# Two-part weights of a hybrid decoder trunk, made by transfers within SBUF

## Chip, cores, metric

One core of a Trainium2 chip runs the whole kernel in one launch. The metric is the device time of that launch in microseconds (us); the kernel before takes 1227.74 us (median of 2 runs, 1227.51 to 1227.97).

## What is computed

The reference is a decoder trunk of two layers on 512 tokens with 1024 features, all in float32:

```
for l in range(DEPTH):                                   # DEPTH = 2
    proj = rms_norm(h, g_mix[l]) @ w_in[l]               # 1024 x 2560: q | k | v | xr | gr
    ... differential attention of 4 heads on q, k, v     -> o
    ... causal convolution, RG-LRU scan on xr, GELU(gr)  -> y
    h = h + concatenate([o, y]) @ w_out[l]               # 1024 x 1024
    hm = rms_norm(h, g_mlp[l])
    h = h + square(relu(hm @ w_mlp_in[l])) @ w_mlp_out[l]    # 1024 x 4096, 4096 x 1024
    gate = sigmoid(rms_norm(h, g_ple[l]) @ w_ple_gate[l])    # 1024 x 1024
    h = h + gate * (p[l] @ w_ple_proj[l])                # 256 x 1024
return rms_norm(h, g_final)
```

## The kernel before

**Numbers in two parts.** TensorE multiplies in the type fp32r, which keeps fewer bits than float32. Every operand is therefore split into a part `hi`, rounded to fp32r, and a part `lo`, the rest. One product of float32 numbers is three fp32r products: hi by hi, hi by lo, lo by hi (`mm3`).

**Weights.** They come as 206 chunks of [128, 1024] float32 (512 KB, 4 KB in each partition), in the order of their use (`chunk_list`): per layer 21 for the input projections and the recurrent gates, 8 for the output projection, 64 for the MLP, 10 for the per-layer embedding. The first two are loaded by halves (`w_half`); the other 204 go through `w_dma`, a load on SP's queue into one of 4 buffers `raw`. `w_split` turns a chunk into `wh` and `wl`, of which there are 6 buffers each. For the chunks of the MLP's first product (`up`) it calls `pair_parts`: that product follows Strassen's method over two output tiles, so VectorE first makes three sums `s1`, `s2`, `s4` of [128, 512] and rewrites half of the second chunk in place; then the two chunks and the three sums are split, the sums into tiles `sh` and `sl` from the general pool of 57 tiles.

In both places ScalarE writes `hi` (a Copy that rounds to fp32r) and VectorE writes `lo = src - hi`. Each chunk's `raw` buffer is free for the next load once `lo` is written, and `wh`, `wl` are free once TensorE has used them.

**Stages of a layer.** x branch (4 chunks and the gates), v (4), four heads (q and k, 8), gate branch (4), output projection (8), then the MLP in four quarters of the hidden features. A quarter has an up stage (8 chunks, 4 pairs, 7 products of halves each) and a down stage (8 chunks, 192 matmuls of 512 columns). The per-layer embedding ends the layer.

**Order.** All instructions are recorded first, with a cost each, and put in order by a list schedule (`Plan.schedule`): each engine takes the oldest recorded instruction that is ready by the modelled times. Every engine's queue, POOL's and SP's among them, then runs in that order, and an instruction that waits holds up what stands behind it on its queue. The plan takes a transfer to occupy its issuing queue 0.47 us and all transfers to share one stream of 355 bytes per ns. All recorded instructions carry line 182 in the profile, so tiles tell them apart. POOL issues no transfer in this kernel; after the set-up it computes the small powers for the norms (`rT`, `orT`).

Of the kernel before, what the change touches and what calls it, by code (L numbers as in the profile page):

```python
# [11 lines left out]
F32 = mybir.dt.float32  # L12
F32R = mybir.dt.float32r
I32 = mybir.dt.int32
AF = mybir.ActivationFunctionType
# [10 lines left out]
NQ = KF // KD  # L26
ORDER = (0, 4, 1, 5, 2, 6, 3, 7)     # output tiles, so that the halves of the features that Strassen pairs come together
HS = S // 2
# [4 lines left out]

# buffers
TB = 57     # tiles of [128, 512]
AT = 2      # tiles for the probabilities of a head, transposed
RAW = 4     # weight chunks as loaded
WB = 6      # weight chunks, split
SC = 4      # PSUM banks that scores may hold

# chunks split ahead in the MLP's products
UA = 2
DA = 2

# the list schedule
WIN = 600   # instructions beyond the oldest one not issued that it may choose from
EV = 150    # boost of what frees PSUM
LP = 600    # how far the norm's sums are put off
RE = -50    # boost of the rotary tables
SW = 2      # us that an instruction waits at most for others that need no new activation table  # L50
SF = 8      # free tiles from which on no check for deadlock is needed
WU = 8      # products that warm up the tensor engine
NM = 4      # output tile of the first up product after which the norm's scale is computed

# [11 lines left out]
class Plan:  # L66
    """Records instructions and issues them in the order of a list schedule: each engine takes, of what is ready,
    what was recorded first (less its boost)."""

# [114 lines left out]
    def schedule(self):  # L184
# [36 lines left out]
        def safe(i):  # L221
            """Whether all that is older than the newest instruction issued can still find its tiles in program order."""
            need = {}
# [132 lines left out]

# columns of the packed per-feature vectors
VCOL = {}
# [16 lines left out]
def chunk_list():  # L375
    """Weight chunks of [128, 1024] in the order in which they are used."""
    c = []
    for l in range(DEPTH):
        c += [("in", l, 12 + m) for m in range(2)]
        c += [("gates", l, 0)]  # L380
        c += [("in", l, 12 + m) for m in range(2, 4)]
        c += [("v", l, i) for i in range(4)]
        for h in range(NH):
            c += [("in", l, h), ("in", l, 4 + h)]
        c += [("in", l, 16 + m) for m in range(4)]
        c += [("out", l, m) for m in ORDER]
        for q in range(NQ):
            c += [("up", l, q * KD + m) for m in range(KD)]
            c += [("down", l, m, q) for m in ORDER]
        c += [("proj", l, 0)]  # L390
        c += [("gate", l, m) for m in range(4)]
        c += [("proj", l, 1)]
        c += [("gate", l, m) for m in range(4, 8)]
    return c
# [6 lines left out]
def build(ctx: ExitStack, tc: tile.TileContext, given, x, p, pos, w, vec, lamqk, out):  # L401
# [25 lines left out]

    # ---------------- weights: streamed, split into two parts that add up exactly
    raw_t, w_t = {}, {}
# [3 lines left out]
    def w_half(i, c):  # L433
        """Half a chunk, for the products that come first."""
        t, hi, lo = T("w0"), T("w0h", F32R), T("w0l", F32R)
        nc.sync.dma_start(out=t, in_=w[i][:, c * S:(c + 1) * S])
        w_t.setdefault(i, []).append((hi, lo))
        nxt["dma"] = nxt["split"] = i + 1
        return t, hi, lo

    def w_dma(j):
        while nxt["dma"] <= min(j, len(CHUNKS) - 1):
# [4 lines left out]
            nxt["dma"] += 1  # L447

    def w_split(j):
        while nxt["split"] <= min(j, len(CHUNKS) - 1):  # L450
# [9 lines left out]
            lo = nc.tile(wsp, [128, 1024], F32R, "wl", WB, "wl")  # L460
            act(out=hi, in_=raw, func=AF.Copy)
            ve.tensor_tensor(out=lo, in0=raw, in1=hi.bitcast(F32), op=ALU.subtract)
            w_t[i] = (hi, lo)
            nxt["split"] += 1

    def pair_parts(a1, a2):
        """The seven weight operands of Strassen's product (Winograd's form) for two output tiles."""
        lft, rgt = slice(0, S), slice(S, 2 * S)
# [6 lines left out]
        for src, n in ((a1, 2), (a2, 2), (s2, 1), (s1, 1), (s4, 1)):  # L475
# [3 lines left out]
            else:  # L479
                hi, lo = T("sh", F32R), T("sl", F32R)  # L480
            act(out=hi, in_=src, func=AF.Copy)
            ve.tensor_tensor(out=lo, in0=src, in1=hi.bitcast(F32), op=ALU.subtract)
            parts += [(hi[:, i * S:(i + 1) * S], lo[:, i * S:(i + 1) * S]) for i in range(n)]
# [22 lines left out]
    def split(src, hi, lo):  # L506
        """src (SBUF or PSUM) into hi + lo."""
        act(out=hi, in_=src, func=AF.Copy)
# [9 lines left out]

    # ---------------- constants
    vt = const.tile([128, NV], F32, name="vt")  # L520
# [21 lines left out]
    def warm_up():  # L542
        """Products of zeros that bring the tensor engine to its full clock while the first loads run."""
        z = T("z", F32R)
# [15 lines left out]
    def rope_setup():  # L560
        """cos and signed sin of the angles, feature-major, 1 and 0 on the rows that don't rotate."""
        posf = T("posf")[:, 0:NT]
# [6 lines left out]
        NA = NT * 16  # L569
        # ang = hi + lo, 1/(2 pi) as a sum of 12-bit parts: every product is exact  # L570
        rest, parts = 1.0 / (2.0 * math.pi), []
# [58 lines left out]
    def vec_setup():  # L630
        for l in range(DEPTH):
            act(out=hb[:, l, 0:4], in_=vt[:, VCOL["b_gate_a", l]:VCOL["b_gate_a", l] + 4], func=AF.Copy, scale=0.5)
            act(out=hb[:, l, 4:8], in_=vt[:, VCOL["b_gate_x", l]:VCOL["b_gate_x", l] + 4], func=AF.Copy, scale=0.5)
            act(out=gsub[:, l:l + 1], in_=V("g_subln", l), func=AF.Copy, scale=1.0 - lam_init(l))
        # softplus(-x) = max(-x, 0) + log1p(exp(-|x|)), the log1p as 2 atanh(y / (2 + y))
        n = DEPTH * 4
# [18 lines left out]
        ve.tensor_scalar(out=sp4n.rearrange("p l t -> p (l t)"), in0=s, scalar1=-4.0, scalar2=None, op0=ALU.mult)  # L655
        # lambda of the differential attention, on every partition
        lq = T("lq")
# [11 lines left out]

    # ---------------- norms: h times its gain goes into the products, 1/rms after them  # L670
    class Norm:
# [20 lines left out]
        def stats(self, square=False):  # L692
            """1/rms (or its square), token-major, and spread over the partitions."""
            ps = PS("msq")
# [24 lines left out]
    class FinalNorm:  # L719
        """The last norm, on each half of the tokens as soon as that is complete."""  # L720

# [35 lines left out]
    def group(ws, rhs, nk, done, late=0, mid=None, tk=slice(0, S)):  # L757
        """ws: per output tile a function giving the chunk slices of K tile k. The last `late` K tiles come last."""
        pss_ = [PM("dense") for _ in ws]
# [16 lines left out]

    # ---------------- one layer
    def layer(l, h, nm, last):
        hg = lambda k: nm.hg[k]
        gate_w = [None]  # L780
        scan_o = [None] * 4
        yo = [None] * KD     # 0..3 attention heads, 4..7 recurrent tiles

# [4 lines left out]

        # recurrent branch
        lru = [dict() for _ in range(4)]  # L790
# [68 lines left out]

        # x branch  # L860
        ws = [take_in(12), take_in(13)]
# [8 lines left out]

        # v, token-major
        pv = [PM("pv") for _ in range(NT)]
# [19 lines left out]

        # attention
        mask_sh = [(i ^ 8) if i < 16 else i for i in range(32)]

        def rope_done(ps, dst):
# [6 lines left out]
            if not dst:  # L903
                # q: per component, its hi part on its own rows and its lo part on the other's
                x0, x1 = T("qx", F32R), T("qx", F32R)
# [5 lines left out]
            else:  # L911
                # k: per component, its hi part on both, and its lo part on its own rows
                y0, y1, lo = T("ky", F32R), T("ky", F32R), T("kl", F32R)
# [115 lines left out]

        # gate branch  # L1030
        for t in range(4):
            group([take_in(16 + t)], hg, KD, lambda i, ps: gr_done(t, ps))

        # output projection; the recurrent tiles come first, the last head last
        order = [4, 5, 6, 7, 0, 1, 2, 3]

        nm2 = Norm("g_mlp", l)
        bp = [dict() for _ in range(4)]     # Strassen's operands of h times its gain, per pair of feature tiles
        fp, t4s = [None] * KD, []
        fat = [AT, []]  # L1040

        def BT(name):
            """512 columns of a tile like those that hold a head's probabilities, as long as there are any."""
            if not fat[1] and fat[0]:
# [40 lines left out]

        # MLP in quarters of the hidden features; the first product by Strassen's method over pairs of output tiles,
        # halves of the input features and halves of the tokens
        nm3 = Norm("g_ple", l)
# [73 lines left out]

        # per-layer embedding
        nmn = None if last else Norm("g_mix", l + 1)
# [18 lines left out]
        def ple(ms, ws, tk, done, **kw):  # L1183
            """proj and gate products of the output tiles ms on the tokens tk."""
            pj = []
# [93 lines left out]
def _layout(i):  # L1279
    """Lays the arrays out as the launch reads them."""  # L1280
    a = {k: np.asarray(v) for k, v in i.items()}
# [59 lines left out]
```

## Time and profile before

| | us |
|---|---|
| median of 2 runs | 1227.74 |
| span of the profiled execution, first to last instruction | 1225.4 |
| PE busy (matmuls) | 1210.8 |
| VectorE busy | 949.0 |
| ScalarE busy | 654.8 |
| POOL busy | 21.4 |

The span is 2.3 us short of the median of the runs; the rest lies around the first and the last instruction. Busy times are those of one profiled execution. A matmul's duration in the profile overlaps the next one's, so the pace of TensorE is read from a stretch and its count of matmuls, not from the mean duration.

### The profile page before, as it was taken

What the parts mean: (1) busy time and instruction counts of PE and PEld (TensorE: products, weight loads), DVE (VectorE), ACT (ScalarE), POOL (GpSimd) and SP (SyncE); (2) the same over time, 40 slices, a digit from 0 to 9 for tenths busy, and PEclk for the clock granted to TensorE, in tenths of its full rate; (3) what the DMA queues carried; (4) which work ended last, traced back from release to release, by engine and by line L of the source; (5) the groups of instructions that cost most, each with busy time, mean ns of one, the idle gap of its engine ahead of it and who ended that gap; (6) DMA issues with size and microseconds to landing.
All of it is one profiled execution on the core that took longest, in us unless ns stands there. A gap on an engine that the chain in (4) does not pass through costs nothing.

```text
span 1225.4 us, 17658 instructions
## 1 busy us (share of the span) xinstructions
PE 1210.8 (99%) x6848; PEld 1049.7 (86%) x6848; DVE 949.0 (77%) x1642; ACT 654.8 (53%) x1068; POOL 21.4 (2%) x43
## 2 busy tenths in 40 slices
PE   8999999999999999999999999999999999999996
PEld 6877788998988989988888777889899899898886
DVE  9898889987777678575778888799776787786564
ACT  6875557743543535543458566576445354355352
POOL 1000000000000000000000000000000000000000
PEclk9999999999999999999999999999999999999998
DMA  6321133243332333332323111223433333343202
GB/s 234 103 69 52 52 89 101 85 124 100 106 103 90 118 93 114 103 103 87 104 69 118 55 35 52 75 81 107 134 103 104 91 104 97 91 136 103 86 1 69
DMA packets 34371, 114.71 MB, mean 94 GB/s; under 512 B 3952, under 2 KB 6000, under 8 KB 34288
## 3 DMA queue, kind: packets, MB, share of 16 engines
q1 hardware_dynamic: 34288, 113.59, 30.2%
q8 instruction: 54, 0.88, 0.3%
q14 instruction: 29, 0.24, 0.1%
HBM read 111.48 MB, written 2.10 MB: 93 GB/s over the span
## 4 chain that ended last, share of the span: by engine, by line
PE 94%; DVE 3%; ACT 1%; DMA 0%; issue 0%; POOL 0%; SPq 0%; POOLq 0%; DVEq 0%; ACTq 0%
PE dense L182 55%; PE up L182 26%; PE sc L182 4%; PE pv L182 2%; PE pj L182 2%; PE av L182 1%; PE bc L182 1%; PE tr L182 1%; PE msq L182 1%; PE osm L182 0%; PE gates L182 0%; DMA h<-x 0%; DVE hs L182 0%; DVE a L182 0%; ACT ky L182 0%
## 5 line engine op out<-in xcount | busy, mean ns | idle before, releaser
L182 ACT ACTIVATE wh<-raw 128x1024 fp32r<-128x1024 f32 x204 | 214.3, 1057 | 279.6 <-PE dense L182 151.8
L182 DVE TENSOR_TENSOR wl<-raw,wh 128x1024 fp32r<-128x1024 f32 x204 | 247.6, 1218 | 22.4 <-ACT wh L182 22.0
L182 PE MATMUL dense<-ffh,wh 128*128 128x512 f32 x512 | 199.5, 390 | 0.0
L182 PE MATMUL dense<-ffl,wh 128*128 128x512 f32 x512 | 199.4, 389 | 0.0
L182 PE MATMUL dense<-ffh,wl 128*128 128x512 f32 x512 | 199.2, 389 | 0.0
L182 PE MATMUL dense<-hgh,wl 128*128 128x512 f32 (+1 forms) x400 | 151.3, 378 | 0.0
L182 PE MATMUL dense<-hgh,wh 128*128 128x512 f32 (+1 forms) x400 | 151.1, 378 | 0.0
L182 PE MATMUL dense<-hgl,wh 128*128 128x512 f32 (+1 forms) x400 | 150.3, 376 | 0.0
L182 PEld LDWEIGHTS dense<-ffh,wl 128*128 128x128 f32 x512 | 96.1, 188 | 20.0
L182 PEld LDWEIGHTS dense<-ffh,wh 128*128 128x128 f32 x512 | 96.1, 188 | 19.8
L182 PEld LDWEIGHTS dense<-ffl,wh 128*128 128x128 f32 x512 | 96.2, 188 | 19.5
L182 ACT ACTIVATE sh<-s 128x512 fp32r<-128x512 f32 x96 | 59.9, 628 | 78.1 <-DVE s L182 77.6
L182 DVE TENSOR_TENSOR dn<-dense,rbc 128x512 f32<-128x512 f32 x64 | 44.2, 690 | 72.7 <-PE dense L182 71.9
L182 PE MATMUL up<-bl,wh 128*128 128x256 f32 x352 | 99.6, 283 | 0.0
L182 PE MATMUL up<-bh,wl 128*128 128x256 f32 x352 | 99.6, 283 | 0.0
L182 PE MATMUL up<-bh,wh 128*128 128x256 f32 x352 | 99.5, 283 | 0.0
L182 PEld LDWEIGHTS dense<-hgl,wh 128*128 128x128 f32 x400 | 75.5, 189 | 12.1
L182 PEld LDWEIGHTS dense<-hgh,wl 128*128 128x128 f32 x400 | 75.5, 189 | 11.9
L182 PEld LDWEIGHTS dense<-hgh,wh 128*128 128x128 f32 x400 | 75.5, 189 | 11.8
L182 PE MATMUL up<-bl,sh 128*128 128x256 f32 x288 | 81.5, 283 | 0.0
L182 PE MATMUL up<-bh,sl 128*128 128x256 f32 x288 | 81.5, 283 | 0.0
L182 PE MATMUL up<-bh,sh 128*128 128x256 f32 x288 | 81.3, 283 | 0.0
(236 smaller groups left out, 2572.0 us busy)
## 6 DMA issues: line engine op xcount, KB each, us to landing
raw<-w SPq DMA_DIRECT2D x204, 512.0 KB, 3.6
h<-x SPq DMA_DIRECT2D x8, 256.0 KB, 5.4
out<-fin SPq DMA_DIRECT2D x8, 256.0 KB, 2.4
w<-w SPq DMA_DIRECT2D x4, 256.0 KB, 4.5
pT<-p SPq DMA_DIRECT2D x4, 256.0 KB, 4.0
lq<-lamqk SPq DMA_DIRECT2D x1, 256.0 KB, 7.1
vt<-vec SPq DMA_DIRECT2D x1, 61.0 KB, 2.4
posi<-pos SPq DMA_DIRECT2D x1, 2.0 KB, 3.0
```

The lines of the kernel that those rows point to most:

```text
L182: d["fn"](*d["args"], **d["kw"])
```

## The change

A new function `w_parts` takes the place of the two instructions of a split, for every chunk and every Strassen sum that was split in `w_split` and `pair_parts`. POOL issues a transfer from the source to `hi` that converts float32 to fp32r; ScalarE writes `lo = -src`, rounded to fp32r; POOL issues a second transfer that adds the source to `lo` in place. VectorE's subtraction is gone. The first two chunks (`w_half`) and all activations keep the old split. The rest of the diff only takes comments away.

```diff
+    def w_parts(src, hi, lo):
+
+        nc.gpsimd.dma_start(out=hi, in_=src)
+        act(out=lo, in_=src, func=AF.Copy, scale=-1.0)
+        nc.gpsimd.dma_start(out=lo.bitcast(F32), in_=src, accum_op=ALU.add)
...
     def w_split(j):
...
             lo = nc.tile(wsp, [128, 1024], F32R, "wl", WB, "wl")
-            act(out=hi, in_=raw, func=AF.Copy)
-            ve.tensor_tensor(out=lo, in0=raw, in1=hi.bitcast(F32), op=ALU.subtract)
+            w_parts(raw, hi, lo)
...
     def pair_parts(a1, a2):
...
                 hi, lo = T("sh", F32R), T("sl", F32R)
-            act(out=hi, in_=src, func=AF.Copy)
-            ve.tensor_tensor(out=lo, in0=src, in1=hi.bitcast(F32), op=ALU.subtract)
+            w_parts(src, hi, lo)
```

## Rows read from the trace of the kernel before

**Rows 1.** The profile's page: busy time of each engine and its share of the span.

```profile
PE 1210.8 (99%) x6848; PEld 1049.7 (86%) x6848; DVE 949.0 (77%) x1642; ACT 654.8 (53%) x1068; POOL 21.4 (2%) x43
```

**Rows 2.** The page: chain that ended last, by engine and by line.

```profile
PE 94%; DVE 3%; ACT 1%; DMA 0%; issue 0%; POOL 0%; SPq 0%; POOLq 0%; DVEq 0%; ACTq 0%
PE dense L182 55%; PE up L182 26%; PE sc L182 4%; PE pv L182 2%; PE pj L182 2%; PE av L182 1%; PE bc L182 1%; PE tr L182 1%; PE msq L182 1%; PE osm L182 0%; PE gates L182 0%; DMA h<-x 0%; DVE hs L182 0%; DVE a L182 0%; ACT ky L182 0%
```

**Rows 3.** Windows: both MLPs whole, then an up and a down stage of layer 0.

```profile
core 0: us, PE busy (x) PEld busy (x) DVE busy (x) ACT busy (x) POOL busy (x), PEclk, DMA share, GB/s
217.77:555.11 337.34, 337.34 (x2130) 307.23 (x2129) 255.65 (x387) 164.53 (x245) 0.00 (x0) 1.00 0.34 105
817.32:1154.57 337.25, 337.25 (x2129) 307.22 (x2129) 255.53 (x386) 165.22 (x245) 0.00 (x0) 1.00 0.34 105
...
303.53:343.84 40.31, 40.31 (x337) 40.31 (x337) 30.53 (x50) 21.57 (x34) 0.00 (x0) 1.00 0.36 111
343.84:387.39 43.55, 43.55 (x194) 36.04 (x194) 31.46 (x43) 17.00 (x24) 0.00 (x0) 1.00 0.29 91
```

**Rows 4.** Groups of instructions: the splits of the weights (busy us, mean ns, idle before).

```profile
L182 DVE TENSOR_TENSOR wl<-raw,wh 128x1024 fp32r<-128x1024 f32 x204 | 247.6, 1218 | 22.4 <-ACT wh L182 22.0
L182 ACT ACTIVATE wh<-raw 128x1024 fp32r<-128x1024 f32 x204 | 214.3, 1057 | 279.6 <-PE dense L182 151.8 <-issue 52.2 <-PE up L182 51.2
L182 DVE TENSOR_TENSOR sl<-s,sh 128x512 fp32r<-128x512 f32 x96 | 63.3, 683 | 0.2
L182 ACT ACTIVATE sh<-s 128x512 fp32r<-128x512 f32 x96 | 59.9, 628 | 78.1 <-DVE s L182 77.6
```

**Rows 5.** DMA of the whole span: packets, MB, share of 16 engines; weight loads.

```profile
q1 hardware_dynamic: 34288, 113.59, 30.2%
...
raw<-w SPq DMA_DIRECT2D x204, 512.0 KB, 3.6
```

**Rows 6.** Windows: the first loads, when many stand in SP's queue at once.

```profile
6.00:20.00 14.00, 12.38 (x47) 8.12 (x47) 13.11 (x23) 13.21 (x25) 0.00 (x0) 1.00 0.96 353
6.00:9.00 3.00, 1.89 (x6) 0.78 (x5) 2.11 (x6) 2.21 (x6) 0.00 (x0) 1.00 1.02 364
12.00:15.00 3.00, 2.84 (x13) 1.97 (x12) 3.00 (x6) 3.00 (x6) 0.00 (x0) 1.00 1.04 407
```

**Rows 7.** What one tile's instructions take (ns): a load's issue, the norms' powers.

```profile
L182 SPq DMA_DIRECT2D raw<-w x204: 327/328/430, 6.7 to 1157.2; - x102
...
L182 POOL TENSOR_TENSOR orT<-ome,mhalf x8: 1006/1166/2917, 116.6 to 780.1; 128x4 f32<-128x4 f32 x8
...
L182 POOL TENSOR_TENSOR rT<-me,mhalf x6: 697/1007/2069, 28.7 to 1217.3; 128x4 f32<-128x4 f32 x4, 128x2 f32<-128x2 f32 x2
```

**Rows 8.** Windows: the four stretches outside the MLPs, and their sum.

```profile
3.00:217.77 214.77, 211.42 (x976) 166.32 (x975) 192.43 (x426) 143.85 (x262) 8.01 (x17) 1.00 0.31 99
555.11:632.00 76.89, 76.89 (x356) 64.17 (x356) 50.09 (x68) 33.34 (x46) 2.01 (x2) 1.00 0.30 90
632.00:817.32 185.32, 184.72 (x864) 147.31 (x863) 157.09 (x308) 121.70 (x222) 6.63 (x4) 1.00 0.23 69
1154.57:1225.40 70.83, 61.58 (x401) 56.19 (x399) 36.40 (x68) 24.84 (x52) 2.40 (x3) 0.94 0.12 38
sum 547.81, PE 534.61 PEld 434.00 DVE 436.00 ACT 323.74 POOL 19.05; mean PE 133.65 PEld 108.50 DVE 109.00 ACT 80.94 POOL 4.76
```

**Rows 9.** Waits of SP's queue: for whom, us in total, times, longest.

```profile
SPq L182 <- DVE wl L182: 1011.6, 186, 20.6
```

**Rows 10.** Windows: the end of the span.

```profile
1210.00:1215.00 5.00, 4.09 (x34) 3.83 (x32) 2.44 (x6) 1.65 (x4) 0.00 (x0) 1.00 0.00 0
1215.00:1225.40 10.40, 2.05 (x10) 1.67 (x10) 3.17 (x7) 0.82 (x2) 0.70 (x1) 0.62 0.30 102
```

## The prediction

> **What bounds the kernel now.** I read the busy times of the engines first: PE is busy 1210.8 us of a span of 1225.4 us, so all that another engine can give back is 14.6 us [rows 1]. The chain that ended last says the same in another way: 94% of it is PE, almost all `dense` and `up` products, 3% VectorE [rows 2]. Then I cut the span into stages. In both MLPs PE is busy in the whole of 337.3 us, at the full clock, so a quarter of an MLP takes 84.3 us, 40.3 of it up and 43.6 down, while VectorE is busy 76% and the DMA engines 34% of the time [rows 3]. So PE's pace is the bound, weights arrive early, and what VectorE does for them is hidden. SP's queue shows how early: it waits 1011.6 us in all for `wl` to release a `raw` buffer [rows 9]; loads are held back, not late.
>
> **What the change takes off.** VectorE loses 204 subtractions of 1.218 us and 96 of 0.683 us, 247.6 + 63.3 = 311 us [rows 4]. All of it lies beside PE, so the gain is bounded by PE's idle 14.6 us, and I take 0: that idle time is mostly the start, the end (9.3 us of it [rows 8]) and the attention's chains, which hold few weight splits. ScalarE keeps 300 instructions of the same shapes, now writing `lo` instead of `hi`; I take their time as unchanged.
>
> **What it adds.** 300 pairs of transfers: 204 of 512 KB and 96 of 256 KB, each once converting and once accumulating. In units of one 512 KB transfer these are 252 and 252, beside 204 loads. Per MLP quarter: 16 loads; 8 down chunks plus 4 pairs of 2 + 3/2 units make 22 conversions and 22 accumulations.
>
> *Price of a unit.* The trace has no transfer within SBUF, so I bound it by loads. Over the whole span 113.59 MB took 30.2% of 16 engines [rows 5]: 370 us, 3.26 us per MB, 1.71 us per unit of 0.524 MB. That is loads coming one at a time. When many were queued at the start, the engines moved 353 GB/s for 14 us at a share of 0.96, 1.485 us per unit, and for 3 us 407 GB/s, 1.29 us [rows 6]. After the change the queues would be full nearly always, so I take the 14 us row, 1.485 us, and keep 1.29 and 1.71 as ends. A conversion between two four-byte types moves what a load moves: one unit. An accumulation writes as much but reads two operands, the source and the old `lo`. Its ends are one unit (if writing decides) and two (if reading does). I take two, since a load's engine is already busy reading as much as it writes.
>
> The Trainium skill, Collectives: The Full Stack, section "The bandwidth ceiling: the fold count and why AG ≠ RS ≠ AR", says that the addition inside a DMA engine is free and that its second read is what halves the rate, with 62.28 against 32.35 GB/s. By that ratio, 1.93, the accumulation would be 1.93 units, and the time 1517 instead of 1536 us; no row of this trace shows it.
>
> *The MLP quarter.* 16 + 22 + 2 x 22 = 82 units, by 1.485 us = 121.8 us of all 16 engines, against 84.3 us of products [rows 3]. That no longer hides. The buffers (4 `raw`, 6 `wh` and `wl`) level out a few chunks, not a quarter, so I count the full difference, 37.5 us, eight times: +300 us. Ends: 60 units by 1.29 = 77.4 us, nothing lost; 82 by 1.71 = 140.2 us, +447 us.
>
> The Trainium skill, DMA: Bandwidth & Descriptors, section "Where 436 GB/s comes from", holds that transfers within SBUF are bound by the fabric, 435 GB/s, and loads by HBM. An estimate from it, 1.20 us for the 66 units that stay in SBUF, gives 103 us a quarter and some 1385 us in all. The highest rate of the trace here, 407 GB/s over 3 us, lies below it [rows 6].
>
> *Outside the MLPs.* 76 units of loads, 76 of conversions and twice 76 for accumulations, 304 by 1.485 = 451 us, fit into the 547.8 us of these stretches [rows 8]. They fit stage by stage too, except the two output projections: 8 chunks of 4 units are 47.5 us, against 43.6 us for 192 matmuls (the down stage's count and pace [rows 3]): +4 us each, +8 us. At 1.71 us a unit it is 520 us, still inside.
>
> *Waits and queues.* POOL's queue gets 600 transfers in order. The accumulating one waits for ScalarE's `lo`; behind it stand the next conversion and, at times, one of the norms' powers (about 1.2 us of work [rows 7]), for which PE's products of the norm wait. A conversion that waits for a `wh` buffer holds both up too. There are 14 such powers (8 `orT`, 6 `rT` [rows 7]); one held up by an accumulation of about 3 us costs up to 40 us in all, but in attention PE has other products to run, so I take 0 and keep +40. SP's loads no longer wait for `wl` from VectorE but for the accumulation: `raw` lives longer by two transfers, roughly 2 x 3.6 us by the landing time of a load [rows 5]. With its own landing, four Strassen sums of some 0.7 us and ScalarE's 1.1 us [rows 4] that makes about 15 us; four buffers then give a chunk every 3.7 us, against 5.0 to 5.4 us that PE needs per chunk [rows 3], so this is not the bound by itself.
>
> **Sum.** Against the profiled span: 1225.4 + 300 + 8 - 0 = 1533 us; the median of the runs lies 2.3 us above the span, so **1536 us**. With the ends of the prices: 1228 to 1683 us, and 40 us more if the powers hold PE up.
>
> **Rivals.**
> *Not slower: the transfers hide.* If an accumulation costs one unit and a unit 1.29 us, a quarter needs 77.4 us against 84.3. This holds up to 1.40 us per unit at 60 units; beyond it each 0.1 us costs 6 us a quarter, 48 us in all. For it speaks the 407 GB/s [rows 6]; against it that the same engines kept it up for 3 us only, and that one pass for three streams would have to be free. The time would be 1213 (all of PE's idle gone) to 1250 us.
>
> *POOL becomes the bound.* It issues 16 transfers in a down stage and 40 in an up stage, 56 a quarter. The nearest rows are SP's issue, 0.33 us, and a POOL instruction, about 1.2 us [rows 7]: 18 to 67 us a quarter, hidden behind the transfers, though the 40 of an up stage at 1.2 us already make 48 us of its 40.3. From 121.8 / 56 = 2.2 us each it decides. If POOL handled one transfer only as fast as a load lands, 3.6 us [rows 5], a quarter took 202 us: +939 us, 2167 us. So 1700 to 2200 us.
>
> *The clock falls.* PE would wait 37 of every 122 us. The trace shows the granted clock below 1 only at the very end, 0.62 while PE was busy 2.05 of 10.4 us; with 1.89 of 3 us busy at the start it stayed at 1.00 [rows 6, 10]. Were the waits enough for the lower of its two levels, 1.2 GHz, throughout, a quarter's products took 168.6 us, more than the transfers: +674 us, about 1900 us.
>
> *Converting or accumulating is far dearer than its bytes*, twice the units of the sum or more: 16 + 44 + 88 = 148 units, 220 us a quarter, +1084 us, above 2300 us with what no longer fits outside the MLPs. Nothing in the trace speaks for or against it.
>
> That the converting transfer copies bits without rounding is possible; it would move the same bytes and change no time.
>
> **How the numbers follow.** The sum's case 0.50 (its own range 1330 to 1690 us), hidden transfers 0.14, POOL 0.19, clock 0.07, far dearer 0.10. A measurement of this kernel can tell about 2% from no change, so 1203 to 1252 us counts as the same: hidden transfers give 0.12 to that and 0.02 to faster, which needs more than PE's idle time. The other cases are all slower: 0.86. The range from 1250 to 2200 us leaves out the hidden ones and the dearest.
>
> **What the changed profile would show.** Right: DMA share near 1.0 in both MLPs, PE busy about 70% there with waits on the two kinds of transfer, a quarter at about 122 us, attention nearly as before, VectorE down by 311 us. A down stage should stay near 44 us when the buffers were full, and an up stage, with 8 + 14 + 28 = 50 units, take up to 74 us. If the DMA share stays near 0.7 with PE waiting, the step on prices is wrong and POOL's queue is where to look: its transfers back to back without a wait. If PE's clock in the MLPs is below 1, the clock's rival holds. If the accumulations land in the time of a conversion, the two units were wrong.

## The result, and the profile after

The changed kernel takes 1501.14 us (median of 2 runs, 1500.07 to 1502.21), 1.2227 times the kernel before, with a 95% interval of 1.2204 to 1.2250. The forecast was 1536 us in a range of 1250 to 2200. The profiled execution has a span of 1498.3 us, 272.9 us more than before.

The profile's page, with the lines that answer to [rows 1, 2, 5]: busy times, the granted clock, DMA share and rate in 40 slices, the DMA queues, the chain that ended last, and the median landing times of the transfers.

```profile
PE 1322.4 (88%) x6848; PEld 1129.4 (75%) x6848; DVE 674.2 (45%) x1342; ACT 646.5 (43%) x1067; POOL 445.4 (30%) x643
...
PEclk9989898998998899799999999999989988989998
DMA  9995489999999999999998945999999999999991
GB/s 304 283 264 141 113 204 258 284 302 261 275 282 280 243 281 291 243 290 292 297 288 225 261 127 145 259 282 291 288 244 268 301 242 261 301 243 285 291 273 56
...
q0 software_dynamic: 86400, 264.28, 72.6%
q1 hardware_dynamic: 34288, 113.59, 21.3%
...
DMA 54%; PE 30%; issue 7%; POOL 5%; ACT 2%; DVE 2%; SPq 0%; POOLq 0%; DVEq 0%; ACTq 0%
...
raw<-w SPq DMA_DIRECT2D x204, 512.0 KB, 7.9
wh<-raw POOLq DMA_DIRECT2D x204, 512.0 KB, 8.8
wl<-raw POOLq DMA_DIRECT2D x204, 512.0 KB, 11.0
```

Read it from the chain: where 94% were PE [rows 2], 54% are now transfers. The DMA row is full but for two valleys, in which the attention of the two layers runs. VectorE's busy time is down by 275 us, and nobody needed them. (The durations of its instructions sum to 311 us less, as forecast; busy time counts stretches in which two of them overlap only once.) POOL is busy 30% of the time, so its issuing is not what fills the span.

The windows by stage answer to [rows 3]; their ends are where the first matmul of a stage starts. The first three are the up, down and up stages of the second and third quarter of layer 0, the last two the MLPs whole.

```profile
343.90:409.93 66.03, 50.05 (x337) 48.01 (x336) 19.99 (x39) 20.66 (x35) 22.95 (x33) 0.87 1.03 265
409.93:455.61 45.68, 43.85 (x194) 35.96 (x193) 13.36 (x21) 14.32 (x18) 14.65 (x21) 1.00 1.03 284
455.61:525.91 70.30, 52.48 (x337) 49.43 (x336) 23.20 (x44) 23.12 (x38) 24.71 (x35) 0.81 0.99 256
238.80:692.63 453.83, 382.28 (x2129) 339.56 (x2128) 162.21 (x290) 167.58 (x256) 154.57 (x217) 0.90 1.04 275
965.88:1418.54 452.66, 380.74 (x2129) 337.92 (x2128) 161.11 (x287) 164.59 (x252) 152.44 (x214) 0.91 1.03 274
```

The MLPs take 906.5 us instead of 674.6 [rows 3], +231.9. All else takes 591.8 instead of 550.8, +41.0. Inside an MLP it is the up stages: 60 to 62 us in the first quarter and 66 to 70 in the others, instead of 40.3, while a down stage is at most 6 us longer. PE's granted clock is 0.90 and 0.91 over the two MLPs, so its busy time rose as well, from 674.6 to 763.0 us. What PE waits for says the same (the view of waits, PE alone: us in total, times, longest):

```profile
PE up L182 <- DMA wl<-raw: 64.5, 35, 3.5
PE up L182 <- DMA sl<-s: 31.2, 20, 4.0
PE dense L182 <- DMA wl<-raw: 16.5, 11, 2.1
```

The waits that sum to most are for the accumulating transfers, `wl` and `sl`, and fall in the up stages.

### The profile page after: what moved, and what is told of

Read it like the earlier page. It is cut to its first block, busy times and chain, and to the rows that moved or that the text cites. A ratio compares the mean times of both kernels' runs of the same rounds, so it can differ in the third digit from the quotient of the medians.

```text
span 1498.3 us, 18971 instructions
## 1 busy us (share of the span) xinstructions
PE 1322.4 (88%) x6848; PEld 1129.4 (75%) x6848; DVE 674.2 (45%) x1342; ACT 646.5 (43%) x1067; POOL 445.4 (30%) x643
## 4 chain that ended last, share of the span: by engine, by line
DMA 54%; PE 30%; issue 7%; POOL 5%; ACT 2%; DVE 2%; SPq 0%; POOLq 0%; DVEq 0%; ACTq 0%
DMA wl<-raw 33%; PE dense L182 16%; DMA raw<-w 15%; PE up L182 5%; PE sc L182 4%; DMA sh<-s 2%; DMA sl<-s 2%; POOL sl L182 1%; POOL wh L182 1%; PE pv L182 1%; POOL wl L182 1%; PE av L182 1%; POOL sh L182 1%; ACT wl L182 1%; PE pj L182 1%
## 5 line engine op out<-in xcount | busy, mean ns | idle before, releaser
L182 ACT ACTIVATE wl<-raw 128x1024 fp32r<-128x1024 f32 x204 | 213.5, 1054 | 284.8 <-DMA raw<-w 217.8
L182 POOL DMA_DIRECT2D wh<-raw x204 | 140.0, 744 | 487.7 <-DMA raw<-w 263.1
L182 POOL DMA_DIRECT2D wl<-raw x204 | 195.4, 1013 | 187.7 <-ACT wl L182 138.3
L182 POOL DMA_DIRECT2D sh<-s x96 | 76.7, 810 | 223.7 <-DVE s L182 191.9
L182 ACT ACTIVATE sl<-s 128x512 fp32r<-128x512 f32 x96 | 58.6, 624 | 145.8 <-DVE s L182 142.2
L182 DVE TENSOR_TENSOR u<-up,p 128x256 f32<-128x256 f32 x32 | 13.6, 424 | 227.2 <-PE up L182 170.1
L182 POOL DMA_DIRECT2D sl<-s x96 | 98.0, 1023 | 59.0 <-DMA wl<-raw 18.1
L182 PE MATMUL up<-bl,wh 128*128 128x256 f32 x352 | 110.4, 314 | 1.8 <-DVE bl L182 1.8
L182 PE MATMUL up<-at,wl 128*128 128x256 f32 x160 | 53.7, 336 | 64.5 <-DMA wl<-raw 64.5
L182 ACT ACTIVATE c<-c 128x512 f32<-128x512 f32 x64 | 39.8, 622 | 135.2 <-DVE c L182 135.2
```

Of the source, the lines that this page charges most:

```text
L182: d["fn"](*d["args"], **d["kw"])
```

## The experiments

My theory: the 16 DMA engines have more to move per MLP quarter than its products last, with an accumulation at twice a conversion's price. Rivals: POOL's queue and the waits in it, whatever the bytes; a clock of PE that falls; buffers that are held too long. Ratios are to the kernel before, with the 95% interval in brackets. The list schedule puts every kernel in order anew, so an edit can shift the order as well; the last run, the kernel before with other buffers, shows 7 us of that kind.

### What a transfer costs by itself

A kernel with none of the trunk's work queues twelve transfers of a kind at once, waits for all, and goes on to the next kind. VectorE notes each landing.

```python
for i in range(N):                       # N = 12; one such loop per kind
    nc.gpsimd.dma_start(out=hi[i], in_=raw[i])                                   # converting
    nc.gpsimd.dma_start(out=lo[i].bitcast(F32), in_=raw[i], accum_op=ALU.add)    # accumulating
    nc.gpsimd.dma_start(out=hi[i].bitcast(F32), in_=raw[i])                      # plain
```

> Computes nothing of the trunk: twelve transfers of each kind, one kind after the other, with a wait for all between. In the changed kernel the POOL queue's transfers take 72.6% of 16 engines for 252 pairs of units of 512 KB, 4.32 us of the engines per pair, and a load 1.48 us. Theory (the addition reads twice): a conversion about 1.45 us and an accumulation about 2.9 us per unit when twelve are queued, a plain transfer within SBUF the same as a conversion. Rival (both kinds are slow because POOL writes their descriptors): both about 2.2 us, the DMA engines idle in between, and plain transfers from POOL equally slow while those from SP take about 1.3 us.

The timeline of VectorE in this kernel, for each kind its first and last regular landing: loads (10 of them, 9 steps), conversions, accumulations, plain transfers from POOL (12 each, 11 steps).

```profile
7.44 0.17 DVE L27 TENSOR_TENSOR mark<-mark,raw 128x8 f32<-128x8 f32 x1 [1.96 <-DMA raw<-w]
...
18.88 0.17 DVE L27 TENSOR_TENSOR mark<-mark,raw 128x8 f32<-128x8 f32 x1 [1.06 <-DMA raw<-w]
...
26.36 0.17 DVE L27 TENSOR_TENSOR mark<-mark,hi 128x8 f32<-128x8 f32 x1 [1.70 <-DMA hi<-raw]
...
42.44 0.17 DVE L27 TENSOR_TENSOR mark<-mark,hi 128x8 f32<-128x8 f32 x1 [1.04 <-DMA hi<-raw]
...
48.38 0.17 DVE L27 TENSOR_TENSOR mark<-mark,lo 128x8 f32<-128x8 f32 x1 [3.52 <-DMA lo<-raw]
...
77.56 0.17 DVE L27 TENSOR_TENSOR mark<-mark,lo 128x8 f32<-128x8 f32 x1 [2.37 <-DMA lo<-raw]
...
81.66 0.17 DVE L27 TENSOR_TENSOR mark<-mark,hi 128x8 f32<-128x8 f32 x1 [1.70 <-DMA hi<-raw]
...
96.57 0.17 DVE L27 TENSOR_TENSOR mark<-mark,hi 128x8 f32<-128x8 f32 x1 [1.09 <-DMA hi<-raw]
```

Per unit: a load (18.88 - 7.44) / 9 = 1.27 us, a conversion (42.44 - 26.36) / 11 = 1.46 us, an accumulation (77.56 - 48.38) / 11 = 2.65 us, a plain transfer from POOL 1.36 us; from SP, by the same reading of this timeline, 1.29 us. The rival wanted both kinds alike at about 2.2 us; they are not: the accumulation costs 1.82 conversions or 1.95 plain transfers. With these prices an MLP quarter is 16 x 1.27 + 22 x 1.46 + 22 x 2.65 = 110.7 us, an up stage 67.7 us and a down stage 43.0 us; the trace of the changed kernel has 66 to 70 and 44 to 49 after the first quarter's. The expectations below were written with 1.40 for the conversion, between the 1.36 of a plain transfer and the 1.46 of a converting one. Each price comes from one run.

A second such kernel asked whether it is the addition or the second read that costs, by accumulating from bfloat16, half the bytes at the source.

```diff
+    nc.gpsimd.dma_start(out=lo[i].bitcast(F32), in_=b16[i], accum_op=ALU.add)
+    nc.gpsimd.dma_start(out=hi[i], in_=b16[i])
```

> Computes nothing of the trunk: ten transfers of a kind, and then ten loads, ten conversions and ten accumulations queued at once. Theory (the reads of the DMA engines set the price, and prices add up): an accumulation from bfloat16 reads three quarters of the bytes of one from float32, 2.0 instead of 2.65 us; the mix takes 10 x (1.27 + 1.40 + 2.65) = 53 us. Rivals: the addition itself is what costs (2.65 us from bfloat16 too), or loads and transfers within SBUF overlap (the mix takes about 40 us).

Again landings in VectorE's timeline: accumulations from float32 (8 steps), from bfloat16 (9), conversions from bfloat16 (9).

```profile
33.78 0.17 DVE L29 TENSOR_TENSOR mark<-mark,lo 128x8 f32<-128x8 f32 x1 [2.38 <-DMA lo<-raw]
...
53.67 0.17 DVE L29 TENSOR_TENSOR mark<-mark,lo 128x8 f32<-128x8 f32 x1 [2.38 <-DMA lo<-raw]
...
58.88 0.17 DVE L29 TENSOR_TENSOR mark<-mark,lo 128x8 f32<-128x8 f32 x1 [2.75 <-DMA lo<-b]
...
77.45 0.17 DVE L29 TENSOR_TENSOR mark<-mark,lo 128x8 f32<-128x8 f32 x1 [1.75 <-DMA lo<-b]
...
81.44 0.17 DVE L29 TENSOR_TENSOR mark<-mark,hi 128x8 f32<-128x8 f32 x1 [1.58 <-DMA hi<-b]
...
92.96 0.17 DVE L29 TENSOR_TENSOR mark<-mark,hi 128x8 f32<-128x8 f32 x1 [1.06 <-DMA hi<-b]
```

From float32 2.49 us, from bfloat16 2.06 us, a conversion from bfloat16 1.28 us. Half the source bytes take 0.42 us off an accumulation, so reading is a good part of its price; 2.06 / 2.49 is 0.83, not the 0.75 that reads alone would give, so they are not all of it; whether the addition itself costs anything stays open. The two readings of an accumulation from float32, 2.65 and 2.49 us, differ by 6%. The mix did not become what it was meant to be: SP's loads ran at the start, and what ran together were 10 conversions, 10 accumulations and 8 stores of half a unit, in 46.9 us (95.16 to 142.05) against 44.6 us by the sum of the single prices (stores priced like loads). Prices add up within about 5% there; whether loads overlap with the others was not measured.

### Bytes against queue

Four kernels leave all else of the changed one and alter `w_parts`.

```diff
 # second transfer without the addition
-        nc.gpsimd.dma_start(out=lo.bitcast(F32), in_=src, accum_op=ALU.add)
+        nc.gpsimd.dma_start(out=lo, in_=src)
```

> The second transfer converts instead of accumulating: as many transfers, bytes written, issues and waits, but no second read; the low part of the weights is then wrong (it repeats the weight). Theory: 60 units of about 1.48 us are 89 us a quarter, 54 us in an up stage against 40.3; about 1300 to 1340 us. Rival (POOL's queue and its waits are the bound, or the granted clock): within 30 us of the changed kernel's 1501 us.

Measured 1293.74 us, 1.0535 (1.0484 to 1.0586). That is 6 us below the theory's range and far from the rival's. Three quarters of the loss, 207 of 273 us, go with the addition and its second read, at the same number of issues and of bytes written. (Transfers also land sooner, a load in 6.2 us by the median instead of 7.9, so a share of what long-held buffers cost is in it.) An up stage should need 8 x 1.27 + 28 x 1.46 = 51.0 us; from the second on they take 47.6 to 52.2 us, the second 47.70 (the windows of this kernel, that up stage and the down stage behind it, where PE never stops):

```profile
309.82:357.52 47.70, 42.82 (x337) 42.01 (x336) 19.99 (x39) 19.32 (x33) 14.68 (x28) 0.96 1.00 333
357.52:401.07 43.55, 43.55 (x194) 36.05 (x193) 16.37 (x26) 17.48 (x23) 12.11 (x24) 1.00 0.94 320
```

```diff
 # only the conversion by transfer
         nc.gpsimd.dma_start(out=hi, in_=src)
-        act(out=lo, in_=src, func=AF.Copy, scale=-1.0)
-        nc.gpsimd.dma_start(out=lo.bitcast(F32), in_=src, accum_op=ALU.add)
+        ve.tensor_tensor(out=lo, in0=src, in1=hi.bitcast(F32), op=ALU.subtract)
```

> Only the high part is made by a transfer, the low part by VectorE as before. Theory: 38 units of about 1.48 us are 56 us a quarter, hidden: 1220 to 1245 us. Rival (each transfer from POOL costs PE something wherever it stands, so half of them cost about half): about 1360 us.

Measured 1249.31 us, 1.0173 (1.0112 to 1.0235), 4 us above the theory's range; the interval takes in 2%. From the second up stage of each layer on, its MLP stages take 40.3 and 43.5 us, as before.

```diff
 # only the accumulation by transfer
-        nc.gpsimd.dma_start(out=hi, in_=src)
+        act(out=hi, in_=src, func=AF.Copy)
```

> The high part by ScalarE as before, the low part by ScalarE's minus and the accumulating transfer, no conversion by transfer. By the prices a quarter needs 16 x 1.27 + 22 x 2.65 = 78.6 us of the engines, less than 84.3, an up stage 47.3 against 40.3 with 12 us idle in the down stage before. Theory: 1235 to 1300 us. Rival (a transfer costs by its wait, not its bytes: half of the 600 are left): about 1360 us.

Measured 1278.39 us, 1.0411 (1.0381 to 1.0441). This kernel gives ScalarE both parts to write; it is busy 248 of the 352 us of the first MLP, so it is not full. Each half alone costs 21 and 51 us, both together 273. That is what two users of one capacity do, with the loss growing once it is full.

```diff
 # all issues, 19.7 instead of 264.3 MB from POOL's queue
-        nc.gpsimd.dma_start(out=hi, in_=src)
-        act(out=lo, in_=src, func=AF.Copy, scale=-1.0)
-        nc.gpsimd.dma_start(out=lo.bitcast(F32), in_=src, accum_op=ALU.add)
+        act(out=hi, in_=src, func=AF.Copy)
+        ve.tensor_tensor(out=lo, in0=src, in1=hi.bitcast(F32), op=ALU.subtract)
+        nc.gpsimd.dma_start(out=hi[:, 0:64], in_=src[:, 0:64])
+        nc.gpsimd.dma_start(out=lo[:, 0:64].bitcast(F32), in_=src[:, 0:64], accum_op=ALU.add)
```

> The old split by ScalarE and VectorE, and behind it both transfers, but of 64 columns only: all 600 issues of POOL and their waits, a tenth of the bytes (the values are off in those columns). Theory (bytes through the engines): 1225 to 1250 us. Rival (POOL's queue, its order and its waits): over 1400 us.

Measured 1248.60 us, 1.0168 (1.0138 to 1.0197). POOL's queue with its 600 issues and their order cost 21 us, not 273; the waits are shorter here, since these transfers land in 2.2 to 3.4 us. Of the 21 us, 15 lie before the first MLP and 5 in the first MLP. In the windows of this kernel PE is idle 3.8 us between 20 and 30 us, where before it had no gap, and runs at a granted clock of 0.56 between 90 and 100 us.

```profile
20.00:30.00 10.00, 6.22 (x19) 4.79 (x19) 9.98 (x57) 2.76 (x4) 4.80 (x5) 0.68 0.51 119
...
90.00:100.00 10.00, 10.00 (x27) 7.36 (x27) 5.89 (x10) 5.46 (x9) 2.33 (x4) 0.56 0.36 105
```

### Place by place

The old split comes back in one of the two callers, or in part of both.

```diff
 # whole chunks the new way, Strassen pairs the old way (in pair_parts)
-            w_parts(src, hi, lo)
+            split(src, hi, lo)
 # Strassen pairs the new way, whole chunks the old way (in w_split)
-            w_parts(raw, hi, lo)
+            split(raw, hi, lo)
 # only chunks outside the MLPs the new way (both edits, this one in w_split)
+            (split if CHUNKS[i][0] == "down" else w_parts)(raw, hi, lo)
```

> The new way for whole chunks (down, and all outside the MLPs), the old split for the Strassen pairs. By the measured prices (load 1.27, conversion 1.40, accumulation 2.65 us a unit) a down stage needs 8 x 5.3 = 42.6 us of the engines against 43.5 us of products, an up stage 8 loads, 10 us. Theory (the engines' time, stage by stage): hidden in the MLPs, 1240 to 1270 us with what the start costs. Rival (every transfer costs PE its share, wherever it stands): 204 of 252 units, about 1450 us.

> The new way for the Strassen pairs alone. Theory: an up stage needs 8 x 1.27 + 14 x 4.05 = 66.9 us, but the down stage before leaves the engines 33 us idle, in which one or two pairs (16.7 us each) are made ahead: 0 to 10 us more in each of 8 up stages, 1235 to 1310 us. Rival (an up stage takes 69 us as in the changed kernel, whatever stands before it): about 1450 us.

> The new way for the chunks outside the MLPs alone, 76 of them. Theory: the MLPs as before, 337 us each; outside the 41 us of the changed kernel, less where that came from a queue still full from an MLP: 1240 to 1268 us. Rival (the 41 us come from the MLPs' queue running over): 1228 to 1235 us.

Measured: whole chunks 1257.13 us, 1.0239 (1.0210 to 1.0269); pairs 1297.24 us, 1.0566 (1.0535 to 1.0597); outside the MLPs 1251.84 us, 1.0196 (1.0152 to 1.0241). All three fall into the theory's ranges, the first two far from the rivals, which put both at about 1450 us; the interval of the third takes in 2%. The sharpest is the first: 280 of the 600 transfers, the down stages' among them, and from the second up stage of each layer on its MLP stages take 40.3 and 43.5 us as before: 43 us of transfers by the prices stand beside 43.5 us of products. In the second, an up stage takes 46 to 53 us instead of 60 to 70, up to 13 us more than before, not up to 10. In the down stage ahead of the second up stage the engines move 247 GB/s at a share of 0.93, as they would if pairs are made ahead. The third shows that of the 41 us outside the MLPs some 24 arise without any MLP transfer: its MLPs take 337.9 and 339.1 us, and in its profiled run 11 us are lost before the first MLP, 14 between the two and none behind the second. At the start PE is idle 3.9 us between 20 and 30 us and 5.5 us between 80 and 90 us, with the DMA share above 1 in both windows (0.39 and 0.35 before).

```profile
20.00:30.00 10.00, 6.07 (x23) 4.25 (x22) 9.13 (x36) 3.83 (x6) 3.84 (x4) 0.85 1.09 313
80.00:90.00 10.00, 4.50 (x20) 3.55 (x18) 5.37 (x9) 5.67 (x8) 2.81 (x4) 0.75 1.07 299
```

### Buffers

The prediction had said that four `raw` buffers are not the bound by themselves.

```diff
-RAW = 4
-TB = 57
+RAW = 6        # and 8 in the next kernel
+TB = 56        # and 52
```

> The changed kernel with 6 buffers for raw chunks instead of 4 (and 56 general tiles instead of 57). Theory (the engines are full): 1480 to 1505 us. Rival (a raw buffer is held too long, through a load and two transfers of 8 to 11 us landing each, so the loads come late): 1350 to 1450 us.

Measured 1427.03 us, 1.1623 (1.1589 to 1.1657): the theory's range was missed, and the rival had 74 us of the 273. The windows over the last three quarters of layer 0's MLP, first of the changed kernel:

```profile
343.90:692.63 348.73, 289.22 (x1585) 255.72 (x1584) 113.19 (x198) 118.13 (x179) 115.72 (x163) 0.89 1.02 271
```

and of the one with six buffers:

```profile
334.91:662.45 327.54, 277.11 (x1585) 245.03 (x1584) 118.53 (x206) 120.24 (x181) 117.80 (x167) 0.94 1.09 293
```

116.2 us a quarter become 109.2, at 293 instead of 271 GB/s. The DMA share of 1.02 had looked like full engines, but the same transfers went faster at 1.09. POOL's waits show what was late, first in the changed kernel:

```profile
POOL wh L182 <- DMA raw<-w: 263.1, 57, 11.3
...
POOL wh L182 <- PE dense L182: 137.2, 32, 9.8
```

then with six buffers:

```profile
POOL wh L182 <- PE dense L182: 215.5, 50, 12.2
...
POOL wh L182 <- DMA raw<-w: 59.7, 23, 10.4
```

With four buffers the conversions stood waiting for loads; with six they wait most for a `wh` that PE still uses. Eight buffers ask whether that is the end of it:

> The changed kernel with 8 raw buffers and 52 general tiles. Theory (6 buffers brought the MLP quarter to 107 us, the sum of the prices is 109 us, so the engines are full): 1410 to 1435 us. Rival (the landing time still holds the loads back): 1340 to 1390 us.

Measured 1436.04 us, 1.1695 (1.1661 to 1.1729), slightly above the theory's range and far from the rival's. The same three quarters take 106.9 us each:

```profile
342.95:663.74 320.79, 277.31 (x1586) 246.57 (x1585) 116.95 (x205) 122.96 (x183) 117.47 (x166) 0.93 1.08 290
```

By the prices it is 110.7 us, or 107.1 us with the 2.49 us that the second price kernel found for an accumulation. So within what the prices are good for, the transfers fill the time. POOL still waits 280.8 us in all for a `wh` that PE uses; more `wh` and `wl` buffers were not tried. What was lost again, against six buffers, lies outside the MLPs; that the five general tiles fewer do it is likely and was not tested.

> The kernel before with 6 raw buffers and 56 general tiles, so that the gain of these buffers is not one that it would have too. Both theories: 1222 to 1235 us.

Measured 1235.29 us, 1.0061 (1.0038 to 1.0083), 0.3 us above what was expected: the kernel before gains nothing from these buffers and loses 7 us. No version with the transfers came below the kernel before; since PE alone fills 1210.8 us of it, none could by more than its idle time.

## Why the prediction held

**What bounds the kernel, and what VectorE's relief is worth**: right. VectorE's 311 us of instructions went and no stage of the MLPs became shorter.

**The mechanism of the sum**: right. The engines' time exceeds the products' in the MLPs, most of all in the up stages ("up to 74 us", measured 60 to 70), and a down stage stays near its own length ("near 44 us", measured 44 to 49). Removing the second read, the conversion, the accumulation or the bytes each took away about what this sum gives for it; two of these four times missed their ranges, by 6 us below and 4 us above.

**The size of the MLP term**: +300 us forecast, +232 measured, from two errors against each other, so that it came this near is in part luck. *The price of a unit*, 1.485 us, was too high for loads (1.27) and for an accumulation (2.97 against 2.65), and nearly right for a conversion (1.46): 121.8 us a quarter in the sum, 110.7 by the measured prices. The 14 us row behind it still held the stretch in which the start's loads ran out; the 407 GB/s row was the nearer one for loads. Two units per accumulation came out as 1.82 conversions or 1.95 plain transfers; with the other reading, 2.49 us, it is 1.71 and 1.83. The ratio in the Trainium skill, Collectives: The Full Stack, section "The bandwidth ceiling: the fold count and why AG ≠ RS ≠ AR", 1.93, lies near the upper end of these, so the measurement agrees with it roughly. The estimate from the Trainium skill, DMA: Bandwidth & Descriptors, section "Where 436 GB/s comes from", 1.20 us a unit within SBUF, was too low for each kind measured (1.29 plain from SP, 1.36 plain from POOL, 1.46 converting); the measurements decide.

*Four raw buffers are no bound* was the step that failed. It counted a lifetime of 15 us with landing times of 3.6 us, those of the kernel before, whose engines are mostly idle. In the changed kernel they are 7.9 us for a load, 8.8 us for a conversion and 11.0 us for an accumulation; the same sum then gives some 32 us, and four buffers a chunk every 7.9 us (an estimate from these medians), where a chunk took 116.2 / 16 = 7.3 us. SP's queue waits for the accumulation to release `raw` (the view of SP's waits, which answers to [rows 9]):

```profile
SPq L182 <- DMA wl<-raw: 1257.3, 200, 21.3
```

This wait alone says little, since it was 1011.6 us when loads were early; that loads are now late shows in POOL's 263.1 us of waiting for them, 59.7 with six buffers. The two MLPs take 853.4 us with six buffers (the windows below) and 841.0 with eight, so of their +232 us 53 to 66 go with this step and 166 to 179 are left for the engines' time.

```profile
236.87:662.45 425.58, 366.81 (x2129) 325.32 (x2128) 164.22 (x294) 168.74 (x258) 153.70 (x217) 0.95 1.09 292
925.89:1353.70 427.81, 368.37 (x2130) 327.20 (x2128) 164.92 (x295) 169.75 (x259) 154.24 (x217) 0.93 1.08 291
```

**Outside the MLPs**: +8 us forecast, +41 measured: 21 before the first MLP, 11 between the two and 9 behind the second (the windows of the changed kernel, which answer to [rows 8]).

```profile
3.00:238.80 235.80, 224.93 (x975) 176.86 (x973) 154.73 (x378) 135.06 (x248) 55.44 (x89) 0.94 0.81 221
692.63:965.88 273.25, 267.59 (x1218) 215.38 (x1216) 162.16 (x323) 149.65 (x258) 68.11 (x95) 0.98 0.85 233
1418.54:1498.31 79.77, 65.31 (x401) 58.45 (x399) 32.16 (x65) 28.35 (x56) 12.47 (x17) 0.89 0.61 175
```

Of the 41 us, PE idles through 18; the other 23 are busy time of the same matmuls, which take longer at a granted clock of 0.94, 0.98 and 0.89 (1.00, 1.00 and 0.94 before). That the transfers "fit stage by stage" did not follow from the prediction's own numbers: a chunk of 4 units at 1.485 us is 5.9 us, more than the 5.4 us of its 24 products, and not in the output projections alone. By the measured prices a chunk of the x and v products needs 5.4 us of the engines for 5.4 us of products. The first loads already fill the engines, so nothing is left to catch up with, and 17 of the first 21 us are lost by 103 us. Some 20 us go with six buffers: the second and third stretch are then about 1 us longer than before, the first still 19. With few bytes the first stretch still loses 15 us, but without the addition, at as many issues and large transfers, only 7. How much of that remainder is POOL's order, landing times or the order that the list schedule chose was not separated.

**Rivals.** *Hidden transfers* fell with the accumulation at 2.65 us. *POOL* fell: an issue takes 0.74 us converting and 1.01 us accumulating on average, below the 2.2 us from which it would decide, and 600 issues with few bytes cost 21 us in all. *Far dearer* fell with the prices. *The clock* fell as the main cause but not as a contribution. Its sign, a clock below 1 in the MLPs, came true without its 1900 us: 0.90 there (0.87 and 0.81 in the two up stages shown) where PE waits, 0.94 with six buffers. No run changed the clock alone. With eight buffers it is still 0.93, while the transfers fill the time by their prices. So by this reckoning the clock can have, of the MLPs' +232 us, at most a share of the 66 us that go with buffers; how much of them is clock and how much is waiting stays open.

## What to carry to other kernels

Moving work from an engine with slack to the DMA engines is not free because they show 34%: count what they would move per stage, with an accumulating transfer as nearly two (1.7 to 1.95 here), and compare with that stage's products, not with the span. When engines fill up, landing times grow: here a load's from 3.6 to 7.9 us, a conversion's from 3.7 us, where it was the only kind from POOL, to 8.8. So every buffer whose release hangs on a transfer has to be counted again with the loaded times. And a DMA share of 1 does not say that the engines move all they could; the rate beside it, for the same mix of transfers, says more (271 GB/s at 1.02, 293 at 1.09).

## What the hardware showed unexpectedly

POOL's queue sends transfers well ahead: ten conversions went out in 5.28 us, the eleventh waited 0.93 us until an earlier one had landed (the timeline of POOL in the first price kernel).

```profile
23.29 5.28 POOL L42 DMA_DIRECT2D hi<-raw  x10
29.50 0.53 POOL L42 DMA_DIRECT2D hi<-raw  x1 [0.93 <-DMA hi<-raw]
```

VectorE's instructions kept their durations while POOL issued 600 transfers: `h<-h,dn` of 128x512 took 688 ns before and 692 ns after, 64 times each. And a transfer within SBUF from POOL, 1.36 us per 512 KB, and 1.29 us from SP, was no faster than a load from HBM, 1.27 us.
